# Weight tiles of an input projection loaded from ScalarE's queue instead of SyncE's

## The chip, the cores and the metric

The kernel runs on one core of one Trainium2 chip. The core has five engines with instruction queues of their own: TensorE (PE: matmuls and, as PEld, weight loads), VectorE (DVE), ScalarE (ACT), GpSimd (POOL) and SyncE (SP), which here does nothing but issue DMAs. An engine takes its instructions in order; one that waits for a semaphore holds all that stand behind it on the same engine. Times are microseconds on the device, from the first instruction to the last. The profile is one execution of the program, with every instruction's start and end.

## What is computed

One step of a decoder layer for a prompt of 1024 tokens and 8 sample tokens that share the weights. One input projection feeds three branches (gated linear attention, causal pooling, cross-attention into 256 memory tokens); each is projected, gated, summed, and one output projection follows. All is float32.

```python
def mixer_layer(x, mem_k, mem_v, S0, pool_hist, pos0,
                w_in, w_a2, b_a, gla_gain, pool_w, pool_scale, w_branch, w_out, norm_gain):
    h = rmsnorm(x, norm_gain)
    proj = h @ w_in
    q, k, v, gla_g, a_lr, u, pool_g, xq, xg, merge = jnp.split(proj, split_pts, axis=-1)
...
    o, S = gla_chunked(q, k, v, log_a, S0)
...
    br_gla = o * jax.nn.silu(gla_g)
    p, new_hist = multiscale_pool(u, pool_hist, pos0, pool_w, pool_scale)
    br_pool = p * jax.nn.silu(pool_g)
    c = cross_attn(xq.reshape(B, T, XA_HEADS, XA_HEAD_DIM), mem_k, mem_v).reshape(B, T, XA_WIDTH)
    br_x = c * jax.nn.silu(xg)
    bproj = jnp.einsum('btnw,nwd->btnd', branches, w_branch)
    gates = jax.nn.sigmoid(merge.astype(jnp.float32)).reshape(B, T, N_BRANCH, D_MODEL)
    merged = jnp.sum(gates * bproj.astype(jnp.float32), axis=2).astype(x.dtype)
    y = merged @ w_out
    return x + y, S.astype(x.dtype), new_hist
```

In cross-attention the prompt attends to memory keys and values that the kernel projects itself; each sample token attends to its own cached keys and values (`cache_mem_k`, `cache_mem_v`), which are read from memory.

## The kernel before

Float32 products are made on TensorE as three products of parts: every operand is split into a high part (rounded to the format fp32r, by ScalarE, line 223) and a low part (the rest, by VectorE, line 224). `mm3` (lines 242 to 244) does high x high, high x low and low x high. Names that end in `h` and `l` are those parts.

The input projection is cut into 40 **pairs**, each 256 columns of `w_in` wide. A pair's weights arrive as two tiles called `raw`, of 512 KB each: `raw[0]` (called the low tile here, `lo` in the code) has rows 0 to 511 of the 256 columns, and `raw[1]` (the high tile, `hi`) rows 512 to 1023. There are three places for `raw` tiles, so that one and a half pairs fit. A pair is computed by seven products in the manner of Strassen, from seven left operands: `a11`, `a12`, `s2`, `s1`, `s3`, `s4`, `a22`. `a11` and `a21` are the halves of the low tile, `a12` and `a22` those of the high one; `s1 = a21 + a22`, `s2 = s1 - a11`, `s3 = a11 - a21` and `s4 = a12 - s2` are made by VectorE in the tile `ws` (line 305; in the trace `ws<-raw`). So the last reader of a low tile is the `ws` of `s3`, and the last reader of a high tile is the split of `a22` (`a22h` on ScalarE, `a22l` on VectorE). A product runs into PSUM banks called `px` (six of them); ScalarE copies some out (`r<-px`, line 554; `c<-px`, line 655), and VectorE adds others up (`c<-px,r`, lines 619, 636, 645).

The list `seq` gives the order of the products: of each pair 1 to 4 (`a12`, `s2`, `s1`, `s3`), then the next pair's 0 (`a11`), then 5 and 6 (`s4`, `a22`). `prepare` makes the operands three products ahead of the one that runs, and it also issues the loads. `fill` puts the rest of the work between the matmuls of the products: up to about 120 us the norm and the memory projection, 120 to 385 us cross-attention (four heads), then linear attention, to about 975 us pooling. After some 1040 us come the branch and output projections, which have weights and loads of their own.

The order on PE and SP is the order of the code. For ScalarE, VectorE and GpSimd the compile-time scheduler of the framework picks an order by its own estimate of when each operand is there; `tc.issue_after(x)` keeps what stands under it behind instruction `x` in that. SP's queue holds, in the order of the code, the `raw` loads and all the other loads that the streams ask for: for a head of cross-attention the queries `xq` of the prompt (line 670), and for the sample group keys `kc` (line 670, two per round), queries spread over the partitions, `qb` (line 767), and values `vc` (line 670).

The sample group's scores go in four rounds per head: a round loads two `kc` tiles and one `qb`, and VectorE reduces four pieces (`kc<-kc,qb`, line 777). The places of these tiles (four, shared by `kc`, `qb` and others) are freed by the round before. The prompt's path in a head: scores in PSUM (`pz`, two places), maximum `nm` (line 709), exponentials and scaling `p` (716), transposes on PE (724), split into `pTh` and `pTl`, and products with the memory values (`mkv`, `mvsh`), whose result ScalarE copies out (`xo`, line 736). `mkTh`, `mkTl` are the parts of the head's transposed memory keys. At the end of a head the sample group's scores are transposed (791), the maximum `nm` is taken (793), normalised (`ps`, 798) and transposed again (803).

Of the kernel before, what the change touches and what calls it, by code (L numbers as in the profile page):

```python
# [18 lines left out]
P = 128  # L19
# [28 lines left out]
def trunk_kernel(ctx: ExitStack, tc: tile.TileContext,  # L48
# [3 lines left out]
    nc = tc.nc  # L52
# [13 lines left out]
    def exp_ln_table():  # L66
        load = nc.scalar.add_instruction(mybir.InstLoadActFuncSet(
            act_func_set_id=EXP_LN_SET, name=nc.get_next_instruction_name(), engine=nc.scalar.engine,
            ins=[], outs=[]))
        for i in table["others"]:  # L70
            tc.add_manual_dep(load.ins, i.ins.name, nosync, reason="table set")
        table["load"], table["others"] = load, []
# [51 lines left out]
    def RAW(name):  # L124
        return wk.tile([P, 4, CT], F32, tag="raw", name=name, bufs=3)
# [92 lines left out]
    last = {}  # L218
# [53 lines left out]
    def load_x(tb):  # L272
        x_t.append(E([D], name=f"x{tb}"))
        nc.sync.dma_start(out=x_t[tb], in_=x_p[tb * P:(tb + 1) * P, :])
# [12 lines left out]
    class Pair:  # L287
# [3 lines left out]
            self.src, self.dst, self.s0, self.gated, self.raw = src, dst, s0, gated, [None, None]  # L291
            self.turned = turned

        def load(self, i):
            raw = RAW("raw")
            nc.sync.dma_start(out=raw, in_=self.src.rearrange("(k p) n -> p k n", p=P)[:, 4 * i:4 * i + 4])
            self.raw[i] = raw

        def operands(self):
# [26 lines left out]
    pairs = []  # L326
# [8 lines left out]
    NPAIR = len(pairs)  # L335
# [12 lines left out]
    def prepare(n):  # L348

        while prep["n"] < min(n + 1, len(seq)):  # L350
            i, j = seq[prep["n"]]
            p = pairs[i]
            if j == 0:
                p.gen = p.operands()
            left[i, j] = next(p.gen)

            if (i, j) == (0, 1):
                pairs[1].load(0)
            if j == 4 and i + 1 < NPAIR:
                pairs[i + 1].load(1)  # L360
            elif j == 6 and i + 2 < NPAIR:
                pairs[i + 2].load(0)
            prep["n"] += 1


# [887 lines left out]
    def emit(n, ahead=AHEAD):  # L1253
        prepare(n + ahead)
        if seq[n] == (28, 0):
            streams[0].rest()
            other_table()
        elif seq[n] == (36, 0):
            streams[1].rest()
        for _ in run_product(n):  # L1260
            fill()
# [10 lines left out]
    for tb in range(4):  # L1272
        load_x(tb)
    next(memory)
    pairs[0].load(0)
    for tb in range(4, 8):
        load_x(tb)
    pairs[0].load(1)

    mem_transposed()  # L1280
    next(memory)
# [18 lines left out]
    with tc.issue_after(last["hi"].ins), tc.issue_after(last["lo"].ins):  # L1300
        prepare(0)
# [6 lines left out]
    with tc.issue_after(last["hi"].ins), tc.issue_after(last["lo"].ins):  # L1308
        prepare(1)
        for j in (4, 6):  # L1310
            r = squares(x_t[j:j + 2], 4 + j)
            scaled(x_t[j], r[:, 0:1])
            scaled(x_t[j + 1], r[:, 1:2], True)
        prepare(3)
# [163 lines left out]
    for hf, order in enumerate(ORDERS):  # L1478
        for tb in order:
# [23 lines left out]
            n, a = hf, 0  # L1503
            for b in ends:
# [14 lines left out]
                n, a = n + 1, b  # L1519
# [46 lines left out]
```

## Time and profile before

| | us |
|---|---|
| median of 3 runs | 1443.5 |
| lowest and highest run | 1441.85 and 1443.95 |
| the profiled execution, its own time | 1445.01 |
| span of that execution, first to last instruction | 1443.3 |
| mean granted TensorE clock | 0.997 |

The span is 1.7 us shorter than that execution's time, since the time has what lies around the program in it too. Rows of the profile read as engine, line, operation and `out<-in` by the program's names. In the timeline a row has start, duration, engine, line, operation and operands; a row with a `q` behind the engine's name (SPq, ACTq) is that engine issuing a DMA, and its duration is the issue and not the transfer. In brackets stands how long the engine was idle before, and what it waited for. The page's share of SP is left out there, because issuing counts as no work.

### The profile page before, as it was taken

The numbers are of one execution on the slowest core, as the hardware profiler recorded it, in microseconds if no ns is written. First come the engines' busy times: TensorE is split into PE (matmuls) and PEld (weight loads), VectorE is DVE, ScalarE is ACT, GpSimd is POOL, SyncE is SP. The second block draws the span as 40 slices with busy tenths as digits, with TensorE's granted clock in tenths as the row PEclk, the third lists the DMA queues.
The fourth block names the chain that finished last, engine by engine and source line by source line (L and its number), as shares of the span: only waits on it lengthen the run. The fifth ranks groups of instructions, "written<-read, shape, count | busy, mean of one in ns | idle before, by whom it ended". The sixth has DMA issues, their size and how long they took to land.

```text
span 1443.3 us, 28179 instructions
## 1 busy us (share of the span) xinstructions
PE 1417.4 (98%) x10689; PEld 1356.1 (94%) x10689; DVE 916.2 (63%) x2123; ACT 679.0 (47%) x1575; POOL 222.1 (15%) x401
## 2 busy tenths in 40 slices
PE   8999999999999999999999999999999999999998
PEld 6899999989899999999999999999999999999876
DVE  6954756666687777767766778785672434554436
ACT  6743544443465666656654445444472432233212
POOL 3211111124342121212221111111010000000000
PEclk9999999999999999999999999999999999999999
DMA  9355665656656363554654455454694777632633
GB/s 329 125 165 169 217 218 187 207 175 165 198 155 193 115 192 129 182 176 126 187 167 150 149 188 170 159 184 163 204 298 134 234 257 249 234 104 79 224 118 116
DMA packets 183507, 259.42 MB, mean 180 GB/s; under 512 B 22204, under 2 KB 132564, under 8 KB 183364
## 3 DMA queue, kind: packets, MB, share of 16 engines
q1 hardware_dynamic: 159900, 183.87, 41.5%
q0 software_dynamic: 23328, 73.56, 14.7%
q8 instruction: 84, 1.38, 0.4%
q14 instruction: 51, 0.42, 0.1%
q10 hardware_dynamic: 144, 0.20, 0.0%
HBM read 180.47 MB, written 77.56 MB: 179 GB/s over the span
## 4 chain that ended last, share of the span: by engine, by line
PE 88%; DMA 5%; DVE 5%; issue 1%; ACT 1%; SPq 0%; POOL 0%; DVEq 0%; ACTq 0%; POOLq 0%
PE px L242 25%; PE px L243 25%; PE px L244 25%; DMA qb<-xqs 3%; PE pz L244 2%; PE pz L243 2%; PE pz L242 2%; DMA raw<-in_w_in_dram 1%; DVE kc L777 1%; PE pz L963 1%; PE pz L404 1%; PE pz L944 1%; PE pz L817 1%; PE pz L946 1%; PE pz L907 0%
## 5 line engine op out<-in xcount | busy, mean ns | idle before, releaser
L244 PE MATMUL px<-bh,wbl 128*128 128x384 f32 (+1 forms) x576 | 184.1, 320 | 0.0
L243 PE MATMUL px<-bl,wbh 128*128 128x384 f32 (+1 forms) x576 | 184.1, 320 | 0.0
L242 PE MATMUL px<-bh,wbh 128*128 128x384 f32 (+1 forms) x576 | 183.7, 319 | 0.0
L554 ACT ACTIVATE r<-px 128x258 f32<-128x258 f32 x240 | 89.9, 375 | 47.4 <-PE px L244 46.9
L242 PEld LDWEIGHTS px<-bh,wbh 128*128 128x128 f32 x576 | 108.3, 188 | 0.0
L243 PEld LDWEIGHTS px<-bl,wbh 128*128 128x128 f32 x576 | 108.2, 188 | 0.0
L244 PEld LDWEIGHTS px<-bh,wbl 128*128 128x128 f32 x576 | 108.2, 188 | 0.0
L242 PE MATMUL px<-ot,s1h 128*128 128x258 f32 x320 | 94.1, 294 | 0.0
L242 PE MATMUL px<-o,a12h 128*128 128x258 f32 x320 | 93.4, 292 | 0.0
L242 PE MATMUL px<-ot,s3h 128*128 128x258 f32 x320 | 93.2, 291 | 0.0
L242 PE MATMUL px<-o,s4h 128*128 128x258 f32 x320 | 93.0, 291 | 0.2 <-DVE c L636 0.2
L242 PE MATMUL px<-o,a11h 128*128 128x258 f32 x320 | 92.8, 290 | 0.0
L242 PE MATMUL px<-ot,a22h 128*128 128x258 f32 x320 | 92.6, 289 | 0.0
L242 PE MATMUL px<-ot,s2h 128*128 128x258 f32 x320 | 92.2, 288 | 0.0
L243 PE MATMUL px<-o,a11h 128*128 128x258 f32 x320 | 91.1, 285 | 0.3 <-DVE o L224 0.3
L243 PE MATMUL px<-o,a12h 128*128 128x258 f32 x320 | 91.1, 285 | 0.0
L244 PE MATMUL px<-o,a12l 128*128 128x258 f32 x320 | 91.0, 284 | 0.0
L244 PE MATMUL px<-ot,s1l 128*128 128x258 f32 x320 | 90.9, 284 | 0.0
L243 PE MATMUL px<-ot,s1h 128*128 128x258 f32 x320 | 90.8, 284 | 0.0
L244 PE MATMUL px<-o,a11l 128*128 128x258 f32 x320 | 90.6, 283 | 0.0
L243 PE MATMUL px<-ot,s2h 128*128 128x258 f32 x320 | 90.1, 281 | 0.5 <-DVE ot L224 0.5
L243 PE MATMUL px<-ot,a22h 128*128 128x258 f32 x320 | 90.5, 283 | 0.0
(471 smaller groups left out, 4634.3 us busy)
## 6 DMA issues: line engine op xcount, KB each, us to landing
raw<-in_w_in_dram SPq DMA_DIRECT2D x80, 512.0 KB, 4.0
msc<-c POOLq DMA_DIRECT2D x24, 516.0 KB, 4.8
brsc<-c POOLq DMA_DIRECT2D x24, 516.0 KB, 3.7
sig<-msc SPq DMA_DIRECT2D x24, 516.0 KB, 6.0
brr<-brsc SPq DMA_DIRECT2D x48, 256.0 KB, 5.2
wbr<-in_w_branch_dram SPq DMA_DIRECT2D x24, 512.0 KB, 5.5
acc<-sig POOLq DMA_DIRECT2D x16, 516.0 KB, 5.2
acc<-acc SPq DMA_DIRECT2D x16, 516.0 KB, 7.0
```

What stands on the lines that cost most here:

```text
L242: nc.tensor.matmul(out, lhsT=lh, rhs=rh, start=start, stop=False, skip_group_check=more)
L243: nc.tensor.matmul(out, lhsT=lh, rhs=rl, start=False, stop=False, skip_group_check=more)
L244: nc.tensor.matmul(out, lhsT=ll, rhs=rh, start=False, stop=stop, skip_group_check=more)
L404: nc.tensor.matmul(t[:, :DV], lhsT=memT[k // 2][:, k % 2, a * P:(a + 1) * P], rhs=raw[k // 2][:, k % 2], start=k == 0, stop=k == NK - 1)
L554: nc.scalar.activation(r, acc[c][:, :QT], AF.Copy)
L777: nc.vector.tensor_tensor_reduce(kc[:, a, :], kc[:, a, :], qb[:, bb, :], scale=1.0, scalar=0.0, op0=ALU.mult, op1=ALU.add, accum_out=sc[:, ...
L817: nc.tensor.matmul(t[32 * j:32 * j + 32, :DV], lhsT=pm[:, a, 4 * i + j, :], rhs=vc[j][:, a, :], start=a == 0, stop=a == 1)
L944: nc.tensor.matmul(t[0:64, 0:P], lhsT=ki[:, 0:64], rhs=qi, start=True, stop=True)
L946: nc.tensor.transpose(t[:, P:2 * P], kt, ident)
L963: nc.tensor.matmul(to, lhsT=kiqi[:, 1, cs], rhs=st, start=False, stop=True)
```

## The change

Of the 80 loads of `raw` tiles three stay on SP: both tiles of pair 0, and the low tile of pair 1. The other 77 go to ScalarE's queue. Where a load stands changes as well: the high tile of the next pair stands behind `s3h` of this pair (`last["hi"]` when product 4 is prepared), and the low tile of the next pair behind `a12h` of this pair (product 1). Before, the low tile was asked for when product 6 of the pair before was prepared, one product earlier.

```diff
-        def load(self, i):
+        def load(self, i, queue=None):
             raw = RAW("raw")
-            nc.sync.dma_start(out=raw, in_=self.src.rearrange("(k p) n -> p k n", p=P)[:, 4 * i:4 * i + 4])
+            (queue or nc.scalar).dma_start(out=raw, in_=self.src.rearrange("(k p) n -> p k n", p=P)[:, 4 * i:4 * i + 4])
             self.raw[i] = raw
...
             if (i, j) == (0, 1):
-                pairs[1].load(0)
-            if j == 4 and i + 1 < NPAIR:
-                pairs[i + 1].load(1)
-            elif j == 6 and i + 2 < NPAIR:
-                pairs[i + 2].load(0)
+                pairs[1].load(0, nc.sync)
+            with tc.issue_after(last["hi"].ins):
+                if j == 4 and i + 1 < NPAIR:
+                    pairs[i + 1].load(1)
+                elif j == 1 and 0 < i < NPAIR - 1:
+                    pairs[i + 1].load(0)
             prep["n"] += 1
...
-    pairs[0].load(0)
+    pairs[0].load(0, nc.sync)
...
-    pairs[0].load(1)
+    pairs[0].load(1, nc.sync)
```

The matmuls and their order on PE stay as they are. On SP the other 526 loads keep their order. Lines behind 363 have a number one higher in the changed kernel.

On SP, head 3's loads of keys and queries for the sample group (`kc`, `qb`) stood so, with the loads of weights between them:

```order
L670 DMA xq<-xqsc_173 128x2x256
L296 DMA raw<-in_w_in_dram 128x4x256
L670 DMA kc<-in_cache_mem_k_dram 128x2x256 x2
L767 DMA qb<-xqs_127 128x512
L670 DMA kc<-in_cache_mem_k_dram 128x2x256 x2
L767 DMA qb<-xqs_127 128x512
L296 DMA raw<-in_w_in_dram 128x4x256
L670 DMA kc<-in_cache_mem_k_dram 128x2x256 x2
L767 DMA qb<-xqs_127 128x512
L670 DMA kc<-in_cache_mem_k_dram 128x2x256 x2
L767 DMA qb<-xqs_127 128x512
L296 DMA raw<-in_w_in_dram 128x4x256
```

In the changed kernel the same place on SP reads:

```order
L671 DMA xq<-xqsc_173 128x2x256
L671 DMA kc<-in_cache_mem_k_dram 128x2x256 x2
L768 DMA qb<-xqs_127 128x512
L671 DMA kc<-in_cache_mem_k_dram 128x2x256 x2
L768 DMA qb<-xqs_127 128x512
L671 DMA kc<-in_cache_mem_k_dram 128x2x256 x2
L768 DMA qb<-xqs_127 128x512
L671 DMA kc<-in_cache_mem_k_dram 128x2x256 x2
L768 DMA qb<-xqs_127 128x512
```

The three `raw` loads are gone from it, and nothing else has moved. They stand on ScalarE now, each behind a split, as here (`a12h`, and two rows later the load):

```order
L223 ACTIVATE a12h<-raw 128x512
L75 ACTIVATE bz<-bz 128x256
L555 ACTIVATE r_6034<-px 128x258
L296 DMA raw<-in_w_in_dram 128x4x256
L75 ACTIVATE bz<-bz 128x256
L555 ACTIVATE r_6059<-px 128x258
```

The scheduler's order on VectorE has moved with it. In head 3, before round 3 of the key reductions (`ISA kc,sc<-kc,qb`), VectorE had these rows; the four reductions of round 3 came behind the last of them:

```order
L224 TENSOR_TENSOR a22l<-raw,a22h 128x512
L709 TENSOR_REDUCE nm<-pz 128x2
L587 STREAM_TRANSPOSE vt<-c_4293 128x512
L714 RECIPROCAL sm<-sm 128x2
L716 TENSOR_SCALAR p<-p,sm 128x256 x2
L636 TENSOR_TENSOR c_4293<-px,r_4475 128x258
L224 TENSOR_TENSOR a12l<-raw,a12h 128x512
L636 TENSOR_TENSOR c_4293<-px,r_4490 128x258
L587 STREAM_TRANSPOSE vt<-c_4293 128x512
```

In the changed kernel the same place on VectorE, from behind `a22l` on, is:

```order
L778 ISA kc,sc<-kc,qb 128x256
L778 ISA sc 128x1
L710 TENSOR_REDUCE nm<-pz 128x2
L778 ISA kc,sc<-kc,qb 128x256
L778 ISA sc 128x1
L588 STREAM_TRANSPOSE vt<-c_4293 128x512
L778 ISA kc,sc<-kc,qb 128x256
L778 ISA sc 128x1
L715 RECIPROCAL sm<-sm 128x2
L778 ISA kc,sc<-kc,qb 128x256
L778 ISA sc 128x1
L717 TENSOR_SCALAR p<-p,sm 128x256 x2
```

Round 3 has moved up, ahead of and between `nm`, `sm` and `p`, and so ahead of the two `c` (line 637 there) that follow. Round 4 has moved up too, ahead of `s2l` and `pTl`; before it stood around `pTl`.

Ahead of head 2's queries VectorE had, behind `a12l`:

```order
L636 TENSOR_TENSOR c_3501<-px,r_3696 128x258
L224 TENSOR_TENSOR mkTl<-pz,mkTh 128x512
L224 TENSOR_TENSOR mkv<-mkv,mvsh 128x512
L224 TENSOR_TENSOR s2l<-ws,s2h 128x512
L777 ISA kc,sc<-kc,qb 128x256
```

In the changed kernel that place on VectorE is:

```order
L637 TENSOR_TENSOR c_3501<-px,r_3694 128x258
L778 ISA kc,sc<-kc,qb 128x256
L778 ISA sc 128x1
L778 ISA kc,sc<-kc,qb 128x256
L778 ISA sc 128x1
L224 TENSOR_TENSOR mkTl<-pz,mkTh 128x512
L224 TENSOR_TENSOR mkv<-mkv,mvsh 128x512
L778 ISA kc,sc<-kc,qb 128x256
L778 ISA sc 128x1
L224 TENSOR_TENSOR s2l<-ws,s2h 128x512
```

Two key reductions of a round have moved in front of `mkTl` and one in front of `s2l`.

## The prediction

> **What bounds the kernel now.** I read the page first, then the waits of PE, then busy time by stretches, and last the timelines of the places where PE stood still. Columns of the page's first row are busy time, share and instructions.
>
> ```profile
> PE 1417.4 (98%) x10689; PEld 1356.1 (94%) x10689; DVE 916.2 (63%) x2123; ACT 679.0 (47%) x1575; POOL 222.1 (15%) x401
> PE 88%; DMA 5%; DVE 5%; issue 1%; ACT 1%; SPq 0%; POOL 0%; DVEq 0%; ACTq 0%; POOLq 0%
> ```
>
> TensorE is busy for 1417.4 of 1443.3 us, and the chain that ends last lies on it for 88%. What a move of loads can win is therefore inside the 25.9 us in which PE is idle, plus what a slow clock costs after an idle. The waits of PE (total, times, longest, in us) tell how that is spread; these are the ones which this change can reach in cross-attention:
>
> ```profile
> PE pz L803 <- DVE ps L798: 2.4, 1, 2.4
> PE pz L243 <- DVE pTl L224: 1.5, 1, 1.5
> PE pz L242 <- ACT xqsh L226: 1.4, 1, 1.4
> PE pz L724 <- ACT xo L736: 1.1, 1, 1.1
> PE pz L791 <- DVE mkTl L224: 1.0, 1, 1.0
> PE pz L242 <- DVE pTl L224: 1.0, 1, 1.0
> ```
>
> The view of busy time by stretches (stretch, length, then PE, PEld, DVE, ACT, POOL, the granted clock, DMA share, GB/s) says where they are:
>
> ```profile
> 120.00:160.00 40.00, 37.44 (x297) 36.78 (x297) 24.37 (x66) 16.17 (x40) 4.60 (x8) 0.96 0.55 172
> 360.00:400.00 40.00, 36.48 (x299) 33.54 (x300) 26.47 (x67) 18.75 (x45) 16.08 (x27) 0.96 0.68 186
> 440.00:1040.00 600.00, 600.00 (x4966) 584.99 (x4966) 433.39 (x1043) 324.59 (x817) 98.70 (x169) 1.00 0.52 165
> 367.00:370.00 3.00, 3.00 (x19) 2.42 (x22) 1.36 (x2) 0.21 (x1) 0.00 (x0) 0.50 0.29 105
> ```
>
> From 440 to 1040 us, where most of the 80 loads are, PE is busy for 600.00 of 600 us: nothing is to be won there, only lost. The gain has to come from cross-attention (120 to 400 us), and of that mostly from its end. There an idle of 2.5 to 3.5 us in 40 is followed by PE at clock 0.50: three microseconds at half speed are 1.5 us of work lost.
>
> **The change part by part.** *SP becomes free.* The waits of SP's own queue show what the loads cost it:
>
> ```profile
> SPq L296 <- DVE a22l L224: 160.3, 20, 12.6
> SPq L296 <- DVE ws L305: 144.0, 20, 10.4
> ```
>
> SP stands for 304 us in front of weight loads whose place is not free, and everything behind them stands too. Most of it harms nobody (PE is full after 440 us). It harms where a load of the sample group's keys and queries is next. That is head 3 (SP's timeline):
>
> ```profile
> 317.05 0.53 SPq L670 DMA_DIRECT2D xq<-xqsc  x1
> 323.90 0.37 SPq L296 DMA_DIRECT2D raw<-in_w_in_dram  x1
> 333.20 0.34 SPq L767 DMA_DIRECT2D qb<-xqs  x1
> 340.54 0.37 SPq L296 DMA_DIRECT2D raw<-in_w_in_dram  x1
> 342.03 0.46 SPq L767 DMA_DIRECT2D qb<-xqs  x1
> 349.32 0.34 SPq L767 DMA_DIRECT2D qb<-xqs  x1
> ```
>
> and VectorE in the same stretch, with the idle before a row and its releaser in brackets; one row of PE and one of ScalarE after it:
>
> ```profile
> 337.24 0.43 DVE L777 CUSTOM_DVE_ANT_0 kc<-kc,qb 128x256 f32<-128x256 f32 x1 [1.86 <-DMA qb<-xqs]
> 340.43 0.69 DVE L709 TENSOR_REDUCE nm<-pz 128x2 f32<-128x512 f32 x1
> 342.95 0.42 DVE L636 TENSOR_TENSOR c<-px,r 128x258 f32<-128x258 f32 x1
> 347.82 0.43 DVE L777 CUSTOM_DVE_ANT_0 kc<-kc,qb 128x256 f32<-128x256 f32 x1 [2.77 <-DMA qb<-xqs]
> 355.06 0.42 DVE L777 CUSTOM_DVE_ANT_0 kc<-kc,qb 128x256 f32<-128x256 f32 x1 [4.10 <-DMA qb<-xqs]
> 355.42 0.69 DVE L224 TENSOR_TENSOR pTl<-pz,pTh 128x512 fp32r<-128x512 f32 x1
> 358.58 0.69 DVE L305 TENSOR_TENSOR ws<-raw 128x512 f32<-128x512 f32 x1
> 363.75 0.69 DVE L305 TENSOR_TENSOR ws<-raw 128x512 f32<-128x512 f32 x1 [2.75 <-issue]
> 346.77 0.28 PE L242 MATMUL px<-o,s4h 128*128 128x258 f32 x1
> 359.31 0.63 ACT L223 ACTIVATE s3h<-ws 128x512 fp32r<-128x512 f32 x1 [5.75 <-DVE ws L305]
> ```
>
> The key reductions come in rounds of four (L777), each behind a `qb`. Before, round 3's `qb` goes out at 342.03 behind the raw load of 340.54, and arrives 5.8 us later (347.82); round 4's goes at 349.32 and arrives at 355.06, after 5.7; round 2's at 333.20 for 337.24, after 4.0. So VectorE comes to `pTl` at 355.42 and PE waits 1.5 us for it; `ws` (L305, s3) is late at 358.58, `s3h` behind it on ScalarE, `xo` behind that (1.1 us of PE); the load which that `ws` frees feeds the `ws` at 363.75, and `ps` is late (2.4 us of PE). This is one chain: the three waits are 5.0 us, and the half clock follows them.
>
> Without raw loads round 1's `qb` can go out soon after `xq` at 317.05 instead of after 323.90, and its reductions stand ahead of the softmax on VectorE, near 327 to 332. The place for round 2's `qb` is then free some 0.9 us sooner than 333.20 and its reductions end at about 338.2 instead of 339.2. Round 3's `qb` then goes at 338.3, not 342.03, and arrives at 342.3 to 344.1 (4.0 to 5.8 after issue). With its four reductions, and `nm`, a transpose and `p` between them, some 2.3 us pass; round 4's `qb` goes at 344.7 to 346.5 and arrives at 348.7 to 352.2. Four reductions (0.35 each), `s2l`, `ws`, `c`, `pTl` (0.6, 0.6, 0.35, 0.6) bring the end of `pTl` to 352.3 to 355.8, against 355.42+0.69=356.1. PE arrives at 356.1-1.5=354.6. **The 1.5 us shrink by 0.3 to 1.5.** `ws` comes 1.1 to 4.6 us earlier than 358.58, so of 1.1+2.4 us for `xo` and `ps` go 1.1 to 3.5.
>
> There is a cost in the same place. The new order has round 3 ahead of `nm` and of `c` (L636, 342.95); `nm` goes from 340.43 to 342.7–344.5, and `c` to 345.5–347.3. PE's product with `s4h` adds into the bank that `c` reads, and starts at 346.77: it waits 0 to 0.9 us. I take -1.0 for `pTl` net of this, -1.0 for `xo`, -2.0 for `ps`. Of the 1.5 us of half clock I take -1.0: once the three waits have gone together, nothing at that place is left to bring it.
>
> *Where reductions have moved in front of `mkTl` (head 2).* SP's row, then VectorE's:
>
> ```profile
> 285.07 0.42 SPq L767 DMA_DIRECT2D qb<-xqs  x1
> 286.76 0.69 DVE L224 TENSOR_TENSOR mkTl<-pz,mkTh 128x512 fp32r<-128x512 f32 x1 [0.78 <-ACT mkTh L223]
> 291.01 0.43 DVE L777 CUSTOM_DVE_ANT_0 kc<-kc,qb 128x256 f32<-128x256 f32 x1 [2.14 <-DMA qb<-xqs]
> ```
>
> Two of round 3's reductions now stand ahead of `mkTl`. This `qb` was not held by a raw load but by round 2 (its place), so it arrives at 290.0 to 291.0 as before. `mkTl`, `mkv`, `s2l`, five 0.35 us steps and `pTl` follow it: 0.6x4+0.35x5=4.1, so `pTl` ends at 294.1 to 295.1. Before, PE waited here until 293.47 (the 1.0 us for `pTl` at L242); now 0.7 to 1.7 us longer. I take **+1.4**, and +0.5 for a half clock that this longer idle may bring (one in three of 1.5).
>
> *The other waits.* `xqsh` (1.4, head 0) hangs on ScalarE, which has one load more ahead of it, and on `xq` loads; 0 is taken, -0.5 to +0.8. `mkTl` in head 0 (1.0) stands behind a `ws` and an `a22l` whose raw load SP issued late, behind a `qb`: -0.5, between -1.0 and 0.
>
> *The start.* These rows are pair 1's high load, the `s3h` it will stand behind, and the VectorE step that reads it:
>
> ```profile
> 36.53 0.37 SPq L296 DMA_DIRECT2D raw<-in_w_in_dram  x1
> 38.54 0.65 ACT L223 ACTIVATE s3h<-ws 128x512 fp32r<-128x512 f32 x1
> 45.48 0.68 DVE L305 TENSOR_TENSOR ws<-raw 128x512 f32<-128x512 f32 x1
> ```
>
> The load goes out some 2.7 us later, behind the `s3h` that ends at 39.19, and the order has its `ws` ahead of the `h` steps (L504) which PE waits for. With 4 us of transfer it lands about when VectorE comes to it: +0.3, from -0.3 to +1.3.
>
> *ScalarE and the steady part.* 77 issues are added to ScalarE. The trace has one issue there, and rows for the slack:
>
> ```profile
> L1528 ACTq DMA_DIRECT2D out_dram<-yl x1: 372/372/372, 1439.5 to 1439.5; - x1
> 984.10 0.63 ACT L223 ACTIVATE a12h<-raw 128x512 fp32r<-128x512 f32 x1 [0.98 <-PE px L243]
> 995.61 0.63 ACT L223 ACTIVATE a11h<-raw 128x512 fp32r<-128x512 f32 x1 [2.02 <-issue]
> DMA to landing us min/median/max: 3.7/4.0/11.9
> ```
>
> 77 x 0.37 = 28.5 us go onto an engine that is idle for 53% of the span; at each place it is 0.37 us in front of an eviction, with six PSUM banks (three products) between PE and a late one. I cost it at nothing; if a quarter of them fell on PE it would be 7 us. The low tile is asked for after `a12h`, one product later than before, and used by `a11h` 10.9 us later (995.61-984.73), against a median landing of 4.0 and a worst of 11.9: nothing, with 1.0 us at worst. The wait that ScalarE takes over is short: the high tile goes behind `s3h`, which reads the very `ws` that frees the place.
>
> A page speaks against the change. The Trainium skill, "DMA: Bandwidth & Descriptors", section "Issuing engines are not separate DMA queues", says that issuing from several engines saves only the sequencer's time to issue, since all transfers share the same 16 engines. By it the sum would be 77 issues that SP does not wait for, and no change. The 304 us of waits in SP's queue speak for more, because here an issue in order waits for a place.
>
> **Sum.** -1.0-1.0-2.0-1.0 (head 3) -0.5 (head 0) +1.4+0.5 (head 2) +0.3 (start) = -3.3 us. Against its own 1445.0 us (span 1443.3) the profiled execution would come to 1441.7; that execution lies 1.5 above the median of 1443.5, and I refer the sum to the median: **1440.2**. About 0.2% (2.9 us) is what a measurement can tell from no change.
>
> **Rivals.** *Only issue time moves.* PE stays bound, head 3's rounds wait for arrivals instead of for SP. (The section of the Trainium skill named above, "Issuing engines are not separate DMA queues", would have this one.) For it: arrivals of 5.7 and 5.8 us with no raw load between round 3 and round 4; at that length `pTl` gains 0.3 and the rest little. Head 3 then gives about -1.5, and with +2.2 and -0.5 the time is 1443.7. Against it: the raw at 340.54 visibly holds the `qb` of 342.03.
>
> *VectorE stands in front of reductions that came forward.* The compile-time order now believes that a `qb` comes early; the engine works in order, so `mkTl`, `nm` and `c` stand behind a transfer. Place: 291 and 343 to 350. Price: +1.7 and 1.5 of half clock in head 2, +0.9 for `c` and +1.0 for `pTl` in head 3, with none of the gains: 5.1 us, 1448.6. It decides from an arrival of about 6.5 us in both rounds of head 3: then `pTl` ends later than 356.1. Against it: no `qb` row above shows more than 5.9.
>
> *ScalarE's own queue blocks.* A load there waits for a place or for an earlier transfer's completion and evictions stand behind it; PE would show waits for `r` or `px` in the full part after 400 us. 40 pairs at 0.1 us are 4 us, 1444.2 with the gains. Against: PE's slack of three products.
>
> **How the numbers follow.** The forecast (head 3 gone, head 2 worse) has 0.55, of which most lies below 1440.6; only issue time 0.22; VectorE in front of reductions 0.13; ScalarE blocking 0.10. The best sum by the bounds is -1.5-3.5-1.5-1.0-0.5+0.7-0.3=-7.6, the worst of the forecast's own +0.5. The range runs from 1435.9 to 1446.5, the upper end half way into the second rival. Faster by over 0.2%: 0.46; within: 0.38; slower: 0.16.
>
> **What would show it.** Right: no SP wait at L296; round 3's `qb` out before 340 and the three waits near 356, 360 and 366 gone or under 1 us together; no half clock at 367; a longer wait near 294 at L242 or L749. Wrong: PE idle between 440 and 1040; ScalarE idle in front of a raw load; waits of PE for `c` L636 above 1 us; key reductions that wait longer for `qb` than before; a new half clock near 295.

## The result, and the profile after

| kernel | median us | runs | ratio to before (95% interval) |
|---|---|---|---|
| before | 1442.64 | 13 | |
| changed | 1448.14 | 13 | 1.0038 (1.0027 to 1.0049) |

The change makes the kernel slower by 0.38%, some 5.5 us; 3.3 us faster was forecast, and the time lies above the range of 1435.9 to 1446.5. Ratios here and below leave out slow runs, of which there were two, 1519.67 us of the kernel before and 1957.49 us of e2. The profiled execution of the changed kernel took 1447.84 us (span 1445.8).

The waits of PE in the changed kernel (total, times, longest), those that answer to the rows of before:

```profile
PE px L495 <- DVE h L505: 4.0, 1, 4.0
PE pz L242 <- ACT xqsh L226: 1.7, 2, 1.4
PE pz L792 <- DVE mkTl L224: 1.5, 1, 1.5
PE pz L804 <- DVE ps L799: 1.4, 1, 1.4
PE pz L750 <- DVE mkTl L224: 1.2, 1, 1.2
PE px L242 <- DVE c L637: 1.1, 2, 0.9
PE pz L242 <- DVE pTl L224: 1.0, 1, 1.0
```

In head 3 the waits for `pTl` (L243) and `xo` are gone, and that for `ps` has fallen from 2.4 to 1.4; all three were to fall by the forecast. The wait for `mkTl` at L750 is new, and that for `c` (L637) has grown from 0.2 to 1.1, also as forecast. The largest of these rows was not forecast: 4.0 us for `h` (L505), at the start. Busy time by stretches of the changed kernel:

```profile
40.00:80.00 40.00, 36.03 (x230) 31.36 (x229) 33.60 (x44) 25.25 (x44) 5.24 (x10) 0.96 0.34 106
48.00:52.00 4.00, 3.21 (x18) 3.12 (x19) 3.97 (x10) 1.12 (x3) 0.00 (x0) 0.71 0.00 0
120.00:160.00 40.00, 37.62 (x297) 36.75 (x296) 26.20 (x64) 16.44 (x41) 4.39 (x8) 0.96 0.56 182
360.00:400.00 40.00, 37.77 (x318) 34.81 (x319) 28.81 (x72) 18.90 (x46) 17.66 (x29) 1.00 0.68 189
440.00:1040.00 600.00, 599.55 (x4962) 584.34 (x4959) 432.13 (x1042) 325.71 (x819) 99.16 (x171) 1.00 0.54 168
```

The half clock of head 3 (360 to 400) is gone from this profile, and one has come at the start (40 to 80, clock 0.71 from 48 to 52). From 440 to 1040 us PE lost 0.45 us in 600: the 51 loads that ScalarE issues from 440 us on cost next to nothing.

The start, in the timelines of ScalarE, then VectorE, then PE of the changed kernel:

```profile
37.67 3.74 ACTq L296 DMA_DIRECT2D raw<-in_w_in_dram  x1
38.20 0.64 ACT L223 ACTIVATE s3h<-ws 128x512 fp32r<-128x512 f32 x1
41.47 1.15 ACT L479 ACTIVATE x<-x,rr 128x1024 f32<-128x1024 f32 x1 [2.63 <-DVE c L620]
42.52 0.61 ACT L223 ACTIVATE a11h<-raw 128x512 fp32r<-128x512 f32 x1
43.17 0.69 DVE L224 TENSOR_TENSOR a11l<-raw,a11h 128x512 fp32r<-128x512 f32 x1 [2.51 <-ACT a11h L223]
47.44 0.69 DVE L305 TENSOR_TENSOR ws<-raw 128x512 f32<-128x512 f32 x1 [3.58 <-DMA raw<-in_w_in_dram]
48.05 0.68 DVE L505 TENSOR_TENSOR h<-px,vec 128x512 f32<-128x512 f32 x1
48.79 2.89 PE L495 MATMUL px<-ident,x 128*128 128x128 f32 x16 [3.96 <-DVE h L505]
```

The issue of one load takes 3.74 us on ScalarE's queue (SP issued the same load in 0.37 in the kernel before). It begins at 37.67, ahead of the start of the `s3h` that stands in front of it in the order, and ends at 41.41; what follows on ScalarE, the scaling of `x` and `a11h`, begins when it is over. (The profile names `c` as the releaser of `x`; that `c` began at 40.24 and took 0.42, so it was done by 40.66, and what held `x` until 41.47 is the issue.) The tile is there at 47.4 us. VectorE has the `ws` that reads it ahead of `h`, stands in it for 3.58 us, and PE waits for `h`.

Head 3 in VectorE's timeline of the changed kernel, the first reduction of rounds 2, 3 and 4 with what stood behind them:

```profile
343.86 0.42 DVE L778 CUSTOM_DVE_ANT_0 kc<-kc,qb 128x256 f32<-128x256 f32 x1 [2.84 <-DMA qb<-xqs]
349.77 0.43 DVE L778 CUSTOM_DVE_ANT_0 kc<-kc,qb 128x256 f32<-128x256 f32 x1 [2.63 <-DMA qb<-xqs]
350.12 0.69 DVE L710 TENSOR_REDUCE nm<-pz 128x2 f32<-128x512 f32 x1
352.99 0.41 DVE L637 TENSOR_TENSOR c<-px,r 128x258 f32<-128x258 f32 x1
356.93 0.43 DVE L778 CUSTOM_DVE_ANT_0 kc<-kc,qb 128x256 f32<-128x256 f32 x1 [1.85 <-DMA qb<-xqs]
359.99 0.68 DVE L224 TENSOR_TENSOR pTl<-pz,pTh 128x512 fp32r<-128x512 f32 x1
```

Round 3 follows round 2 after 5.9 us instead of 10.6, and round 4 after 7.2, as before. It is the mechanism that was forecast: round 3's `qb` no longer waits behind a raw load. But round 1's does not go out soon after `xq`, as the forecast had it: on SP, `xq` goes at 322.71 and the `qb` at 329.52, 6.8 us later (8.4 before), because the `kc` in front of it waits for a place. And the total wait of VectorE for `qb` has not become smaller; the first row is before, the second the changed kernel (waits of VectorE):

```profile
DVE kc L777 <- DMA qb<-xqs: 24.2, 11, 4.1
```

```profile
DVE kc L778 <- DMA qb<-xqs: 27.7, 12, 4.7
```

### The profile page after: what moved, and what is told of

Same layout as the page of the kernel before. It is cut to its first block, busy times and chain, and to the rows that moved or that the text cites. A ratio compares the mean times of both kernels' runs of the same rounds, so it can differ in the third digit from the quotient of the medians.

```text
span 1445.8 us, 28168 instructions
## 1 busy us (share of the span) xinstructions
PE 1418.0 (98%) x10689; PEld 1356.7 (94%) x10689; DVE 915.4 (63%) x2123; ACT 679.5 (47%) x1575; POOL 220.7 (15%) x401
## 4 chain that ended last, share of the span: by engine, by line
PE 73%; DMA 2%; DVE 2%; issue 1%; ACT 0%; POOL 0%; SPq 0%; DVEq 0%; ACTq 0%; POOLq 0%
PE px L242 22%; PE px L243 22%; PE px L244 22%; DMA qb<-xqs 1%; PE pz L243 1%; PE pz L242 1%; PE pz L244 1%; PE pz L964 1%; DMA raw<-in_w_in_dram 1%; PE pz L945 1%; PE pz L947 1%; PE pz L908 0%; DMA mixsc<-xo 0%; PE pz L818 0%; PE pz L1049 0%
## 5 line engine op out<-in xcount | busy, mean ns | idle before, releaser
L243 PE MATMUL px<-bl,wbh 128*128 128x384 f32 (+1 forms) x576 | 184.0, 320 | 0.0
L243 PEld LDWEIGHTS px<-bl,wbh 128*128 128x128 f32 x576 | 108.2, 188 | 0.0
L242 PE MATMUL px<-ot,s3h 128*128 128x258 f32 x320 | 93.2, 291 | 0.0
L242 PE MATMUL px<-ot,s2h 128*128 128x258 f32 x320 | 92.2, 288 | 0.0
L243 PE MATMUL px<-o,a11h 128*128 128x258 f32 x320 | 91.0, 284 | 0.3 <-DVE o L224 0.3
L243 PE MATMUL px<-o,a12h 128*128 128x258 f32 x320 | 90.9, 284 | 0.0
L243 PE MATMUL px<-ot,a22h 128*128 128x258 f32 x320 | 90.5, 283 | 0.0
L244 PE MATMUL px<-ot,s3l 128*128 128x258 f32 x320 | 90.4, 283 | 0.0
L243 PE MATMUL px<-ot,s3h 128*128 128x258 f32 x320 | 90.4, 282 | 0.0
L243 PE MATMUL px<-ot,s1h 128*128 128x258 f32 x320 | 90.4, 282 | 0.0
```

Source lines behind the costliest of these rows:

```text
L242: nc.tensor.matmul(out, lhsT=lh, rhs=rh, start=start, stop=False, skip_group_check=more)
L243: nc.tensor.matmul(out, lhsT=lh, rhs=rl, start=False, stop=False, skip_group_check=more)
L244: nc.tensor.matmul(out, lhsT=ll, rhs=rh, start=False, stop=stop, skip_group_check=more)
```

## Where the time went, matmul by matmul

PE's instructions are the same 10689 in the same order in every kernel here, so the start of the n-th one can be compared between traces. The table gives by how many us a matmul starts later (+) or earlier (-) than in the second profile of the kernel before (e0, below, 1442.47 us), at places named by their time there. It is worked out from the traces of one execution each, which need not be a typical one: that of e3 (1442.95 us) is the slowest of its runs and 3.4 above their median, that of e5 is 2.2 above and that of e1 1.5 above.

| at | before, 1st profile | changed | e1 | e3 | e5 | e7 | e9 | e10 |
|---|---|---|---|---|---|---|---|---|
| 44, start | +0.1 | -0.3 | +0.5 | -0.2 | -0.1 | +0.4 | -0.4 | +0.0 |
| 120, before head 0 | +0.1 | +4.0 | +0.4 | -0.3 | +1.8 | +0.4 | -0.4 | +3.3 |
| 200, behind head 0 | +0.1 | +5.0 | +1.5 | +1.4 | +1.0 | -1.0 | -2.8 | +2.3 |
| 296, head 2 | +0.8 | +7.1 | +3.3 | +2.1 | +3.5 | -1.6 | -3.4 | +1.7 |
| 340, head 3 | +1.9 | +7.5 | +3.9 | +2.0 | +7.3 | -0.9 | -3.4 | +5.4 |
| 350, head 3 | +1.9 | +8.7 | +4.6 | +2.1 | +8.4 | -0.9 | -3.4 | +5.4 |
| 395, behind head 3 | +2.1 | +4.4 | +1.7 | -0.1 | +3.9 | -5.5 | -8.8 | -0.2 |
| 1440, end | +2.5 | +5.0 | +2.6 | +0.2 | +5.1 | -5.1 | -7.9 | +0.4 |

In the changed kernel the start loses 4.0, heads 0 to 2 lose another 3.5, the `c` of head 3 1.1, the rest of head 3 wins 4.3 back, and the later part adds 0.7.

## The experiments

Two theories stood after the result: A, the loss is made at the start, by one load; B, it is spread over the 77 issues. As the runs came in, a third was formed: D, VectorE's order, with key reductions ahead of steps that PE waits for, is what costs in cross-attention.

**e1: the changed kernel with pair 1's high tile back on SP.**

```diff
-                    pairs[i + 1].load(1)
+                    pairs[i + 1].load(1, nc.sync if i == 0 else None)
```

> The changed kernel with one load put back on SP: the high tile of pair 1 (the load that goes out behind s3h near 38 us). Theory A (the loss is made at the start: VectorE stands in ws for that tile until 47.4 us, PE idles 4.0 us for h and then runs at half clock): 4.6 us of the 5.5 come back, 1443 to 1444, PE's wait at L495 under 1 us and no half clock near 48 us. Theory B (the loss is spread: issues on ScalarE, or waits in its queue, in the whole input projection): 1447 to 1448 as before this edit.

1443.96 us, ratio 1.0010 (0.9999 to 1.0021), within what theory A asked for. 4.2 us came back from one load, the wait for `h` is gone, and so is the half clock at the start. The issue of the raw loads, first in the changed kernel, then here (count, then duration in ns: least, median, most):

```profile
L296 ACTq DMA_DIRECT2D raw<-in_w_in_dram x77: 374/374/3742, 37.7 to 1035.9; - x77
```

```profile
L296 ACTq DMA_DIRECT2D raw<-in_w_in_dram x76: 374/374/438, 74.5 to 1033.2; - x76
```

Of 77 issues one was long. Here the first on that queue comes at 74.5 us and is short, so that a first use of the queue is not by itself long. At 38 us the DMA engines are busy (share 1.13 from 38.00 to 41.40 in the changed kernel), but SP's short issue at 36.5 us in the kernel before also stood among busy ones (0.91 from 36 to 38), so that this alone does not explain it either. A holds, B falls.

**e2: the kernel before with that one load on ScalarE, behind `s3h`.**

```diff
             if j == 4 and i + 1 < NPAIR:
-                pairs[i + 1].load(1)
+                with tc.issue_after(last["hi"].ins):
+                    pairs[i + 1].load(1, nc.scalar if i == 0 else None)
```

> The kernel before with one load moved: the high tile of pair 1 on ScalarE's queue behind s3h; all others on SP. VectorE's order keeps ws behind the first two h steps here. Theory A1 (what costs is ws standing ahead of h on VectorE): the late tile costs at most 1.9 us, 1442.6 to 1444.5. Theory A2 (what costs is the issue of 3.7 us that holds ScalarE, and the tile that lands near 47 us, whatever the order): PE loses 3 us and gets the half clock, 1446 to 1447.5. Theory B: 1442.6, nothing.

1448.41 us, ratio 1.0041 (1.0027 to 1.0054): one load out of 80 loses as much as the change. Not all of this is located: the profiled execution is the fastest of the runs (1444.49 us), and in it a matmul at 120 us is 3.2 late, of which 1.9 come back by 200. The time is above every range of the expectation, which was also wrong in one thing: the scheduler put `ws` ahead of `h` here too, as VectorE's timeline of this kernel shows, so that A1 and A2 are not told apart by it.

```profile
46.99 0.69 DVE L305 TENSOR_TENSOR ws<-raw 128x512 f32<-128x512 f32 x1 [2.40 <-DMA raw<-in_w_in_dram]
47.60 0.68 DVE L505 TENSOR_TENSOR h<-px,vec 128x512 f32<-128x512 f32 x1
```

**e3: all loads on SP, at the places of the changed kernel.**

```diff
-            (queue or nc.scalar).dma_start(out=raw, in_=self.src...)
+            nc.sync.dma_start(out=raw, in_=self.src...)
```

> All loads on SP, but at the places of the changed kernel (low tile one product later, in SP's order of the code). Theory Q (what the change does in head 3 comes from the queue): the three waits of PE at 356, 360 and 366 us stay, start as before, 1442 to 1443.5. Theory P (it comes from the place of the low tile's load): the waits in head 3 shrink, 1440 to 1441.5.

1439.55 us, ratio 0.9975 (0.9964 to 0.9986): faster than before, by the place of the low tile's load and what the scheduler makes of it (on VectorE, three of round 3's reductions in head 3 move ahead of `p` and `c`). It is somewhat faster than theory P asked for. In head 3 that load now stands behind round 3's `qb`, and PE's waits for `pTl` and `xo` go without a second queue. What was taken for the effect of the queue can be had by one product's shift on SP. And e1, which differs from e3 in the queue of 76 loads and in the order on VectorE, is 0.35% slower than it; e7 and e8 tell the two apart in part.

**e5: the changed kernel, with the `ws` of pair 1's `s1` kept behind two `h` steps.**

```diff
-            s1 = of(a21, a22, ALU.add)
+            with tc.issue_after(last["hv"].ins) if self is pairs[1] else ExitStack():
+                s1 = of(a21, a22, ALU.add)
...
+                if g == 2:
+                    last["hv"] = hv
```

> The changed kernel with one step of VectorE held back: the ws of s1 of pair 1 is kept behind the first two h steps, where it stood before the change; the load stays on ScalarE. Theory A1 (order of ws): PE's wait at L495 falls from 4.0 to 1.5 or less, no half clock near 48 us, 1443.5 to 1445. Theory A2 (the long issue and the late tile): 1447 to 1448. Theory B (spread): 1447 to 1448, with the wait at L495 gone.

1445.78 us, ratio 1.0025 (1.0014 to 1.0036), between the two theories; the wait for `h` fell to 0.8 us and the start's loss to 1.8 (table). So the order of this one step is about half of the loss at the start, and the rest is not.

**e0: the kernel before, for a second profile.**

> The kernel before, unchanged, for a second profile of it. The first one (1445.0 us) lies above the median of its runs (1442.2 to 1442.6). If what differs from execution to execution is the idle and the half-clock stretches of cross-attention, this one, if faster, has fewer of them between 120 and 400 us, and the same start and the same part after 400 us.

1442.47 us, span 1440.8, against 1445.0 of the first profile. Its stretches:

```profile
120.00:160.00 40.00, 37.33 (x308) 36.66 (x308) 24.04 (x66) 16.05 (x40) 4.24 (x8) 1.00 0.57 172
360.00:400.00 40.00, 37.02 (x302) 33.95 (x302) 26.42 (x67) 19.48 (x49) 13.84 (x23) 0.96 0.64 182
```

The start and the part after 400 us agree within 0.5 us (table). The half clock of head 0 is missing here, with as much idle as in the first profile (37.33 against 37.44 busy); that of head 3 is in both (0.96 from 360 to 400). A single half clock is therefore no sure part of a kernel's time, and a difference of 2 us between two profiles is no finding.

**e6: the changed kernel with the load one row later on ScalarE, behind the scaling of `x`.**

```diff
-            with tc.issue_after(last["hi"].ins):
+            with tc.issue_after(last["hi"].ins), tc.issue_after((last["sx"] if (i, j) == (0, 4) else last["hi"]).ins):
...
-            nc.scalar.activation(x, x, AF.Copy, scale=r[:m])
+            last["sx"] = nc.scalar.activation(x, x, AF.Copy, scale=r[:m])
```

> The changed kernel with pair 1's high load still on ScalarE, but one row later: behind the scaling of x that PE's transposes (L495) wait for. VectorE's order is that of the changed kernel (ws ahead of h). Theory A2 (the issue holds ScalarE while the DMA engines are full): issue at about 39.5, still until some 41.4, x no longer late by 2.1 us, but a11h and the tile as late as before; PE's wait at L495 3 to 4 us because of ws, 1446 to 1448. If the hold of x was all: wait under 1.5 us, 1443.5 to 1445.

1448.39 us, ratio 1.0042 (1.0026 to 1.0058). `x` was on time and nothing was won: the wait for `h` is 3.5 us. With `ws` ahead of `h`, the hold of `x` does not matter.

**e12: e5 and e6 together.**

> e5 and e6 together: pair 1's high load on ScalarE behind the scaling of x, and the ws that reads it behind the first two h steps. Theory: at the start two things cost, the ws that stands ahead of h, and the issue that holds ScalarE for some 4 us ahead of x and a11h. With both out of the way the start loses under 1.5 us against before (the tile still lands near 47 us): 1443.5 to 1445. If the late tile alone keeps VectorE: as e5, 1445.5 to 1447.

1446.48 us, ratio 1.0028 (1.0018 to 1.0037), as e5. In this kernel `x` is on time, and `ws` behind two `h` steps, but the tile still lands only at 47 us, and the next two `h` stand behind `ws` (ScalarE's row, then VectorE's):

```profile
39.09 3.16 ACTq L296 DMA_DIRECT2D raw<-in_w_in_dram  x1
47.09 0.69 DVE L305 TENSOR_TENSOR ws<-raw 128x512 f32<-128x512 f32 x1 [1.75 <-DMA raw<-in_w_in_dram]
47.69 1.28 DVE L506 TENSOR_TENSOR h<-px,vec 128x512 f32<-128x512 f32 x2
```

Before, that `ws` ran at 45.48 without a wait and the two `h` at 46.08: the late tile is 1.6 us on the chain. With that the start is accounted for in the traces: about 1.7 us for a tile that lands near 47, some 2.3 for `ws` ahead of `h` with the idle and the half clock that it brings, and nothing for the hold of `x`. The second theory of the expectation was right.

**e7: e1, with every key reduction kept behind the latest low split in the order of the code.**

```diff
+                    with tc.issue_after(last["lo"].ins):
-                    nc.vector.tensor_tensor_reduce(kc[:, a, :], kc[:, a, :], qb[:, bb, :],
+                        nc.vector.tensor_tensor_reduce(kc[:, a, :], kc[:, a, :], qb[:, bb, :],
```

> e1 (77 loads less one on ScalarE, start on SP), and each key reduction is kept behind the latest low split in the order of the code, so that VectorE no longer has them ahead of mkTl, nm and c. Theory D (the rest of the loss of the ScalarE kernels against e3 is VectorE's order): PE's waits for mkTl at L750 and for c at L637 go, 2 to 3 us faster than e1, 1440.5 to 1442. Theory Q (a queue of its own makes the other loads slower): no faster than e1, 1443.5 to 1445.

1436.52 us, ratio 0.9960 (0.9947 to 0.9972), against 1.0010 for e1: 7.4 us from the order of VectorE alone, more than the 2 to 3 that theory D had asked for.

**e8: e3 with the same edit.**

> e3 (all loads on SP at the new places) with the same hold of the key reductions. Theory D: little to win, since e3 has few reductions ahead of mkTl; 1438.5 to 1440. If the hold delays rounds that head 3 waits for: 1441 to 1443.

1436.31 us, ratio 0.9960 (0.9947 to 0.9972), faster than either theory had it. With the start on SP and the reductions held in both, ScalarE's queue (e7) and SP's (e8) give the same time. VectorE's order is not the same in both: the scheduler set some twenty other steps differently in cross-attention and some hundreds later, mostly where PE is full.

The time is the same, but the landing is not. These rows are for the raw loads issued from 100 to 400 us, first in e7, then in e8:

```profile
DMA to landing us min/median/max: 3.8/5.4/10.1
```

```profile
DMA to landing us min/median/max: 3.6/4.5/6.5
```

The kernel before has 4.1 and at most 5.7 in that stretch, the changed kernel 5.3 and up to 9.0. On ScalarE's queue the loads go out among SP's other loads and land later there; why was not tested.

**e9: the kernel before with the same edit.**

> The kernel before (all loads on SP at the old places) with each key reduction kept behind the latest low split. Theory D1 (the hold of the reductions is the whole gain of e7 and e8, and moving loads adds nothing): as e7 and e8, 1436 to 1437.5. Theory D2 (loads out of SP's way or one product later add to it): head 3 keeps its late qb behind a raw load and waits there, 1439 to 1441.5.

1434.62 us, ratio 0.9947 (0.9935 to 0.9960), the fastest kernel of the study, with no load moved. The time is below both ranges, and nearer to D1's: moving loads adds nothing to it. Head 2 shows what the edit does. VectorE's rows, first in the changed kernel, then in e9:

```profile
295.44 0.43 DVE L778 CUSTOM_DVE_ANT_0 kc<-kc,qb 128x256 f32<-128x256 f32 x1 [3.78 <-DMA qb<-xqs]
295.79 0.42 DVE L778 CUSTOM_DVE_ANT_0 kc<-kc,qb 128x256 f32<-128x256 f32 x1
296.13 0.69 DVE L224 TENSOR_TENSOR mkTl<-pz,mkTh 128x512 fp32r<-128x512 f32 x1
```

```profile
283.83 0.69 DVE L224 TENSOR_TENSOR mkTl<-pz,mkTh 128x512 fp32r<-128x512 f32 x1 [0.95 <-ACT mkTh L223]
287.14 0.69 DVE L224 TENSOR_TENSOR pTl<-pz,pTh 128x512 fp32r<-128x512 f32 x1
287.75 0.42 DVE L778 CUSTOM_DVE_ANT_0 kc<-kc,qb 128x256 f32<-128x256 f32 x1
```

In the changed kernel `mkTl` stands for 3.78 us behind a reduction whose `qb` is on its way; in e9 `mkTl` and `pTl` go first and the reduction then finds its `qb` there. In the stretches of e9 head 2 is full, and head 3 shows no half clock:

```profile
280.00:320.00 40.00, 40.00 (x349) 38.32 (x348) 26.73 (x64) 19.09 (x45) 10.11 (x17) 1.00 0.64 193
360.00:400.00 40.00, 38.99 (x321) 36.42 (x320) 30.12 (x79) 22.74 (x55) 16.49 (x27) 1.00 0.57 149
```

Against e0 head 2 is not where most of the gain lies: the table puts 2.4 us of it in head 0 and 5.4 in head 3. There, in the kernel before, `pTl` (355.42) stood behind a reduction that waited 4.10 us for its `qb`. In e9 `pTl` goes first, and round 4's reductions wait for almost nothing:

```profile
344.27 0.69 DVE L224 TENSOR_TENSOR pTl<-pz,pTh 128x512 fp32r<-128x512 f32 x1 [0.15 <-ACT pTh L223]
350.02 0.42 DVE L778 CUSTOM_DVE_ANT_0 kc<-kc,qb 128x256 f32<-128x256 f32 x1 [0.16 <-DMA qb<-xqs]
```

VectorE's wait for `qb` in all, 24.2 us in the kernel before, is in e9:

```profile
DVE kc L778 <- DMA qb<-xqs: 7.8, 6, 2.8
```

SP still stands 146.7 and 130.6 us in front of raw loads in e9, by its queue's waits, and of PE's waits from 335 to 365 us only 0.3 for `ps` is left: SP's stand costs next to nothing there once VectorE no longer stands in front of what SP brings late.

**e10: the changed kernel, start included, with the same edit.**

> The changed kernel as it is, start included, with the same hold of the key reductions. If the loss of the change is two independent parts (the start some 4 us, the order of the reductions some 5 to 7 us), this is e7 plus the start: 1440 to 1441.5. If the start's delay is taken up later once the order is repaired: 1436.5 to 1438.

1442.49 us, ratio 0.9998 (0.9989 to 1.0007), 1 us above the range for two independent parts. It is 6.0 us above e7, from which it differs in one load. The loss at the start stays to the end; nothing takes it up later. But in the traces it is only 2.9 of what parts the two; another 2.9 come at the end of head 2. There a raw load that ScalarE issues at 297.6 lands after 10.3 us (8.9 in e7, 3.7 in e8 on SP), VectorE stands in front of its reader for 5.3, PE waits 2.1 for `pm` (0.7 in e7), and a half clock follows. It is the pattern of the start once more; whether one brings the other, or this execution was an unlucky one, is not shown.

## Why the prediction was wrong

**The start was mis-sized; this is the step that failed.** "+0.3, from -0.3 to +1.3" became 4.0 us in the trace and 4.2 in the medians (changed against e1); in e2, where nothing else is moved, it is 3.2 in the trace. The prediction had both parts, the tile that goes out later and the `ws` that stands ahead of `h`, and put two sizes in: an issue of 0.37 us, from the only issue on ScalarE in the trace (at 1439 us, with idle DMA engines), and a landing after the median of 4 us, to which the steady part gives most loads. The rows for this place were in the trace: the raw loads issued at 18.3 and 25.4 us landed 11.9 and 9.8 us later, and SP's raw loads at 11.0 and 25.4 took 1.93 and 1.28 us to issue. The load went out 1.1 us later than before and not 2.7, but with 9 us from 38, `ws` is ready at 47, which is what came. VectorE's steps to `h` stand behind it by 3.6 us, and a half clock follows the idle. With 4.0 in place of 0.3 the sum is +0.4 instead of -3.3. The table ends at +5.0, so other terms were short too: heads 0 to 2 lost 3.5 where +1.4 was forecast, head 3 won 3.2 where 5.0 was, and the later part lost 0.7 where nothing was.

**Head 3 was right in mechanism, smaller in size.** The forecast was -5.0 net, with `c` included; the table has -3.2 (+1.1 for `c`, -4.3). The wait for `c` was 0.9, within the 0 to 0.9 given; `pTl` and `xo` went; `ps` kept 1.4 us of 2.4, where 0.4 was left by the forecast. Counted against PE's matmuls, round 3's `qb` went out 1.7 us sooner, and not 3.7, since round 2's went 0.8 later and not 0.9 sooner. The half clock near 367 is gone here, as forecast, but e1's profile, with the same loads in head 3, has it (0.96 from 360 to 400), so that its going is not sure.

**Head 2 was right:** the forecast was +1.4, and it is 2.1 in the table against e0 and 1.4 against the first profile; the half clock that had +0.5 did not come. **Head 0 was wrong in sign:** the wait for `mkTl` at its end grew from 1.0 to 1.5 instead of falling by 0.5; e0 has 1.8 there in the kernel before, so this is no finding.

**The rival that came nearest** is the second, VectorE in front of reductions that came forward. It was given 0.13 and 1448.6, and placed in heads 2 and 3 without the start; that its time is close to 1448.14 is luck. Two signs that the prediction named as wrong came with it: waits for `c` above 1 us in all (1.1), and key reductions that wait longer for `qb` (27.7 against 24.2). VectorE in front of reductions does cost: e7 takes 7.4 us from e1. But that lies in the kernel before already: the same edit wins 7.7 there (e9, 1434.62 against 1442.34). So the change added little of it; it is the start which turned the sign.

**Only issue time moves.** The rule of the Trainium skill ("DMA: Bandwidth & Descriptors", section "Issuing engines are not separate DMA queues") fits the times of e7 and e8, which have the same ratio with 76 loads on one queue or the other. Its remark that an issue is usually small beside the transfer did not hold at 38 us, where the issue took 3.74 of 9.7 us.

**The steady part was right:** 0.45 us lost in 600. The wait of ScalarE for places cost nothing that can be seen.

**Not settled:** why that issue lasts 3.2 to 4.9 us on ScalarE when SP issues the same load in 0.37 at 36.5 us, and whether an issue on ScalarE at 36.5 would also be short, which was not tried. Nor is it known why raw loads on ScalarE's queue land later in cross-attention, and what the rest of e2's loss is. Where in head 0 and head 1 e7 and e9 differ (1.8 us by 200) lies within what single profiles differ by.

## What to carry to other kernels

Price a moved DMA by the rows of its own place: how long issues and landings take in that stretch of the trace, not the median of the run. Before moving loads out of an engine's queue because it stands in it, look which engine stands in front of what comes late; holding the key reductions back on the in-order engine was worth 0.5% here, and another queue for 76 loads nothing. After a change, read the order of every engine that the scheduler sets, since an earlier load makes it put its reader earlier too, whether or not the load is there by then.

## What was not expected of the hardware

An issue on ScalarE's queue took 3.7 to 4.9 us in the kernels whose raw load was issued there near 38 us behind `s3h`, and held ScalarE's next instructions, while all 76 others took 0.37 to 0.45. Begun a little later (38.7 in e6, 39.1 in e12) it took 3.69 and 3.16, and in all six kernels it ended between 41.4 and 42.7 us, as if it waited for something that came free then; what, is not shown. And the clock: in head 0 PE idles for 1.39 us and, 0.5 us later, for 0.3 in all 13 profiles. In six a stretch of 3.41 us at half clock follows, in the other seven none; the two profiles of the kernel before differ in this (0.96 against 1.00 in 120 to 160 us). The Trainium skill, "TensorE: Matmul & The Clock Gate", section "Part 1: The HAM clock gate", says of the window in which activity is counted that it runs free, so that the same kernel differs from run to run; these two profiles agree with it.
